# A hybrid mixer and mixture-of-experts layer on one core: one row load, wider matmul operands, other PSUM banks, and a new order of the last outputs

## The chip, the cores and the metric

The kernel runs on one core of one Trainium2 chip. The core has five engines that are told apart below: TensorE (PE; its weight loads are PEld), VectorE (DVE), ScalarE (ACT), GpSimd (POOL) and SyncE (SP), which here mostly issues DMAs. The metric is the device time of one execution, in microseconds; lower is better.

## The reference

The reference is one layer over 512 latent tokens and 256 context tokens, each of 1024 float32 numbers, written for a depth of 1 and a batch of 1:

- Modulation: `silu(c) @ ada_w + ada_b` gives six rows of 1024 (shift, scale and gate, twice); the context has its own.
- `xm = rmsnorm(x) * (1 + scale) + shift`, and one input projection `p = xm @ w_in` for all branches.
- Branch A: a bidirectional chunked state-space scan (16 heads, 4 groups, chunks of 128 tokens) over `silu(conv(p))`, started from the final states of the context. Its output gets the skip `y + d_skip[head] * xh`, is gated by `silu(z)` and normalised in groups of 256.
- Branch B: `u, v = gelu(uv)`; `v` is layer-normalised and mixed over 128 positions by `w_s`, then multiplied with `u`.
- `merged = sigmoid(gate_a) * (A @ w_pa) + sigmoid(gate_b) * (B @ w_pb)`, and `h = x + g1 * (merged @ w_o)`.
- `xf = rmsnorm(h) * (1 + scale2) + shift2`; each of 16 experts takes its 64 best tokens (`top_k` over a softmax of router logits), computes `silu(xg @ w_gate) * (xg @ w_up) @ w_down`, weighted by the affinity, and adds the result to its tokens: `h = h + g2 * sum`.
- The output is `rmsnorm(h) * final_norm_w`.

All weights are float32; the experts' alone are 16 x 3 x 4 MB = 201 MB.

## The kernel before, in words

**Order.** The work is written down stage by stage for all engines; a scheduler then turns it into one queue per engine, by the order of the program, by priorities and by when it reckons that operands are there. `keep_in_program_order` (the local `matmul` and `transpose`, L1042 to L1047) and `issue_after` (L1158) fix parts of TensorE's order by hand. A tile that is taken again under the same name waits until all that used its buffer is through; `bufs` gives the number of buffers.

**Start (L81 to L347).** POOL loads small rows through its own DMA queue (`vr`, `alog`, `dtb`, and `dsk`, L130: `d_skip` is spread so that partition p of column k has the value of head 2k + p // 64; each of the two loads takes every second of 16 numbers to 64 partitions). SP loads the tokens (L96), then `ada_w` and `w_in` tiles in turn. TensorE starts with `gemv(0)` (L237), which needs the first `ada_w` tile, then transposes the normalised tokens (L255) and projects group 0.

**Precision.** A float32 operand is split into a high and a low float32r part (`split`, L72: a ScalarE copy and a DVE subtraction); a product is three float32r matmuls (L358 to L360, L601 to L603). Products with plain float32 operands appear as two records each in the trace.

**Groups, v and u.** For groups 1 to 3 (L567) TensorE projects while the scan of the group before runs in steps (`ssd_group`, L446). The v half of branch B is projected with tokens on the partitions (`token_major`, L583): four blocks of 256 columns, each in two halves of four k, four token tiles with an accumulator each (`acc`, four banks), and an evacuation `v_out` (GELU by `gelu2`, L608, and `bn_stats`) after the second half. The statistics and the normalisation follow (L632 to L636). Then the scan's memory is given back, and in it `w_s` is loaded and transposed (L751, L760). The u half, the gates and the two branch projections follow (`cols`, `block`).

**Output projection.** `token_major` again (L951) with `w_o`; its evacuation `residual` (L916) multiplies with the gate into the buffer `t0` (one buffer), adds x into `h`, and squares with a sum. Between the halves stand the router's weights and the logits of each 256 columns (`logits`, L925). Softmax and ranking follow (L974 to L1039).

**Experts (L1127).** 16 experts run as 8 pairs, side by side in TensorE's columns. SP streams the weights in 1 MB tiles through 19 buffers (`expert_slots`, L645; `piece`, L687, takes one and issues more loads). Per pair: gate projection (tile `pg`, two PSUM banks), up projection (`pu`, two banks), the gather of the next pair's tokens (`channels`, L1074, two halves that share one tile of two banks, `pu` for the first pair and `pg` for the others), transposes through `x` (two banks), and the down projection in column cuts through `pd` (two banks). The result of a pair is spread to its tokens beside the next pair's gate projection (`to_their_tokens`, L1115).

**The end.** The last pair has cuts of 512, 384 and 128 columns (`LAST`, L29). Their results are spread through the four banks of `pg` and `pu`, the last cut's through `x` (`banks`, L1171); they are added to `h` and squared (L1190 to L1195, with junk output in two weight buffers). Then the final norm: `rsqrt` in nine small DVE steps (L132), `final_norm_w` spread over the partitions by eight matmuls with a broadcast column (L1230), and eight passes of 512 columns on DVE with a store each (L1237, L1238).

Of the kernel before, what the change touches and what calls it, by code (L numbers as in the profile page):

```python
# [18 lines left out]
GELU_K = 0.044715  # L19
# [9 lines left out]
LAST = ((0, 512, 4), (512, 896, 4), (896, 1024, 4))  # L29
# [4 lines left out]
def tile_backbone(  # L34
# [548 lines left out]
    def token_major(src, n0, lh, ll, evac, wt=lambda nb: wtile()):  # L583

        def weights():
            for nb in range(4):
                w = wt(nb).rearrange("p (k n) -> p k n", k=NK)
                load(w, w_cols(src, n0 + 256 * nb, 256))
                for kh in range(2):
                    wh, wl = hl_tile(4, 256)  # L590
                    wsplit(wh, wl, w[:, 4 * kh:4 * kh + 4, :])
                    yield nb, kh, wh, wl

        for nb, kh, wh, wl in ahead(weights()):
            if kh == 0:
                pp = [acc()[:, :256] for _ in range(NT)]
            for t in range(NT):
                for k in range(4):
                    kt = 4 * kh + k
                    a = slice(128 * t, 128 * t + 128)  # L600
                    T.matmul(pp[t], lh[:, kt, a], wh[:, k, :], start=kt == 0, stop=False)  # L601
                    T.matmul(pp[t], ll[:, kt, a], wh[:, k, :], start=False, stop=False)  # L602
                    T.matmul(pp[t], lh[:, kt, a], wl[:, k, :], start=False, stop=kt == NK - 1)  # L603
                if kh == 1:
                    evac(nb, t, pp[t])
            yield
# [12 lines left out]
    def v_out(nb, t, p):  # L619
        a = sp.tile([128, 512], F32, name="tm")[:, :256]  # L620
        gelu2(vt[:, t, 256 * nb:256 * nb + 256], p, a)
        if nb % 2:
            V.bn_stats(bn[:, t, nb // 2, :], vt[:, t, 256 * nb - 256:256 * nb + 256])

    for _ in token_major(W, 4128, xmh, xml, v_out):
        steps(scans, 2)
# [289 lines left out]
    def residual(nb, t, p):  # L916
        cs = slice(256 * nb, 256 * nb + 256)
        a = half("t0", 256)
        V.tensor_mul(a, p, g1b[:, cs])
        V.tensor_add(h[:, t, cs], a, x2[:, t, cs])  # L920
        S.activation(a, h[:, t, cs], AF.Square, accum_out=ssq[:, t, nb:nb + 1])
# [29 lines left out]
    for i, _ in enumerate(token_major(w_o.rearrange("l k n -> (l k) n"), 0, mgh, mgl, residual)):  # L951
        if i in {0:11}:
            fetch({0:11}[i])
        if i == 0:
            router_weights()
# [7 lines left out]
        elif i % 2 == 0:  # L963
            logits(i // 2 - 1)
    logits(3)
# [108 lines left out]
    def channels(xt_, ot, hf, p):  # L1074

        for j in range(4):
# [29 lines left out]
    first_banks = pw.tile([128, 2, 512], F32, name="pu", bufs=1)  # L1106
    for hf in range(2):
        channels(xg, ot, hf, first_banks[:, hf, :])
# [18 lines left out]
    for pr in range(NE // 2):  # L1127
# [15 lines left out]
        if not last:  # L1143
            gather = pw.tile([128, 2, 512], F32, name="pg", bufs=1)
            channels(xg, ot, 0, gather[:, 0, :])
# [6 lines left out]
        if not last:  # L1152
            channels(xg, ot, 1, gather[:, 1, :])
        def down(c0, c1, nk, behind=None):
            pd = pw.tile([128, 512], F32, name="pd", bufs=2)[:, :c1 - c0]
            for k0 in range(0, NK, nk):
                w = [piece() for _ in range(2)]
                with tc.issue_after(behind.ins) if behind and (k0 or c0 > 512) else nullcontext():  # L1158
                    for k in range(nk):
                        kt = k0 + k  # L1160
                        for e in range(2):
                            (T.matmul if last else matmul)(pd[64 * e:64 * e + 64, :], ht[:, kt, 64 * e:64 * e + 64], w[e][:, k, :],
                                     start=kt == 0, stop=kt == NK - 1)
# [7 lines left out]
        def banks(i):  # L1171

            if i == len(LAST) - 1:
                p = pw.tile([128, 512], F32, name="x").rearrange("p (t n) -> p t n", t=NT)
                return [p[:, t, :] for t in range(NT)]
            pp = [pw.tile([128, 2, 512], F32, name=n, bufs=1) for n in ("pg", "pu")]
            return [pp[t // 2][:, t % 2, :] for t in range(NT)]

        def scatter_last(i, a):

            c0, c1, _ = LAST[i]
            pp = banks(i)
            for t in range(NT):
                o = oh[:, 128 * t:128 * t + 128]
# [84 lines left out]
```

## Time and profile before

| | before |
|---|---|
| runs, us | 1151.94, 1154.35, 1153.66 (median 1153.66) |
| profiled execution, us | 1151.37 |
| its span, us | 1149.6 |
| mean granted TensorE clock | 0.989 |
| PE busy, us | 1070.2 (93%) |
| DVE / ACT / POOL busy, us | 579.2 / 331.9 / 66.2 |
| DMA | 291.85 MB, mean 254 GB/s |

The span runs from the first to the last instruction that the profiler saw; the execution's own time has some 2 us around it. Busy shares are averages over stages with different limits, so they are read stage by stage. The ends of matmuls are modelled; what a matmul takes in a stream is read from start to start.

### The profile page before, as it was taken

To read this page: it belongs to the slowest core of one execution; us is meant where nothing else is said; L and a number is where in the kernel's file an instruction comes from. 1 tells how busy PE (TensorE), PEld (TensorE's weight loads), DVE (VectorE), ACT (ScalarE), POOL (GpSimd) and SP (SyncE) were. 2 spreads that over 40 slices of the span, in tenths; PEclk is the share of its full clock that TensorE was granted. 3 is DMA by queue.
4 is the path that set the end of the run, shared out by engine and by line. 5 is a ranking of instruction groups with operands and counts; after the bars stand their busy time and mean duration, and the time that the engine had idled before them with its cause. 6 is when DMAs were issued, how large, how long until landed. Compare 5 with 4: busy or idle time off the path is not lost.

```text
span 1149.6 us, 15045 instructions
## 1 busy us (share of the span) xinstructions
PE 1070.2 (93%) x5939; PEld 709.5 (62%) x5939; DVE 579.2 (50%) x1061; ACT 331.9 (29%) x645; POOL 66.2 (6%) x58
## 2 busy tenths in 40 slices
PE   2999898999999999999999699999999999999985
PEld 1778777789888888777798545353535353535333
DVE  2768999998698565645653630303030303030305
ACT  4344756554343223323333211010101010101002
POOL 2002231321000000100000000000000000000000
PEclk9999999999999999999999799999999999999998
DMA  9941634231476566622464669999999999999994
GB/s 209 255 132 40 206 101 152 93 87 61 144 263 213 187 221 191 211 86 98 147 259 163 238 238 409 393 408 397 404 401 400 406 395 410 391 409 392 409 393 144
DMA packets 149663, 291.85 MB, mean 254 GB/s; under 512 B 8468, under 2 KB 75188, under 8 KB 149592
## 3 DMA queue, kind: packets, MB, share of 16 engines
q1 hardware_dynamic: 149224, 290.79, 70.5%
q0 software_dynamic: 288, 0.07, 0.7%
q8 instruction: 47, 0.77, 0.3%
q14 instruction: 24, 0.20, 0.1%
q10 hardware_dynamic: 80, 0.02, 0.0%
HBM read 288.67 MB, written 2.18 MB: 253 GB/s over the span
## 4 chain that ended last, share of the span: by engine, by line
PE 74%; DVE 11%; DMA 7%; ACT 4%; issue 3%; POOL 1%; SPq 0%; DVEq 0%; ACTq 0%; POOLq 0%
PE pg L1044 15%; PE pu L1044 10%; PE pd L1044 8%; PE acc L358 7%; PE acc L360 7%; PE acc L359 7%; PE x L1044 4%; PE acc L603 2%; PE acc L601 2%; PE acc L602 2%; DMA w<-in_w_up_dram 2%; DMA aw<-in_ada_w_dram 2%; DVE wl L74 1%; ACT m L1083 1%; DVE gq L515 1%
## 5 line engine op out<-in xcount | busy, mean ns | idle before, releaser
L358 PE MATMUL acc<-xmh,wh 128*128 128x512 f32 x352 | 139.0, 395 | 0.0
L359 PE MATMUL acc<-xml,wh 128*128 128x512 f32 x352 | 138.7, 394 | 0.0
L360 PE MATMUL acc<-xmh,wl 128*128 128x512 f32 x352 | 138.1, 392 | 0.0
L73 ACT CAST wh<-w 128x1024 fp32r<-128x1024 f32 (+1 forms) x84 | 84.4, 1006 | 170.4 <-PE acc L359 133.2
L74 DVE TENSOR_TENSOR wl<-w,wh 128x1024 fp32r<-128x1024 f32 (+1 forms) x81 | 96.3, 1190 | 68.0 <-ACT wh L73 66.8
L1168 DVE SCALAR_TENSOR_TENSOR t<-pd,gi,m 128x512 f32<-128x512 f32 (+2 forms) x17 | 12.2, 719 | 151.6 <-PE pd L1044 137.8
L1123 DVE TENSOR_TENSOR F<-F,x 128x512 f32<-128x512 f32 x56 | 38.5, 687 | 91.3 <-PE x L1044 91.3
L1044 PE MATMUL pg<-e,m 128*64 128x512 f32 x296 | 76.0, 602 | 0.0
L1044 PE MATMUL pu<-e,m 128*64 128x512 f32 x304 | 74.8, 595 | 0.9 <-DMA e<-in_w_up_dram 0.9
L360 PEld LDWEIGHTS acc<-xmh,wl 128*128 128x128 f32 x352 | 66.2, 188 | 14.8 <-issue 1.2
L358 PEld LDWEIGHTS acc<-xmh,wh 128*128 128x128 f32 x352 | 66.2, 188 | 14.6 <-ACT wh L73 0.8
L601 PE MATMUL acc<-wh,xmh 128*128 128x256 f32 x256 | 73.6, 288 | 1.0 <-DVE F L614 1.0
L359 PEld LDWEIGHTS acc<-xml,wh 128*128 128x128 f32 x352 | 66.3, 188 | 13.2 <-issue 0.4
L603 PE MATMUL acc<-wl,xmh 128*128 128x256 f32 x256 | 73.4, 287 | 0.6 <-DVE wl L74 0.6
L602 PE MATMUL acc<-wh,xml 128*128 128x256 f32 x256 | 72.6, 284 | 0.0
L1044 PE MATMUL pd<-e,m 128*64 128x512 f32 x280 | 66.6, 594 | 0.0
L1139 DVE TENSOR_TENSOR t<-t,pu 128x512 f32<-128x512 f32 x16 | 10.3, 683 | 99.6 <-PE pu L1044 99.6
L1083 ACT ACTIVATE m<-pg,mcol 128x128 f32<-128x128 f32 x56 | 21.0, 456 | 135.9 <-PE pg L1044 135.9
L1044 PEld LDWEIGHTS pg<-ot,F 128*128 128x128 f32 x448 | 51.1, 192 | 12.5 <-ACT m L1083 6.8
L1044 PE MATMUL pg<-ot,F 128*128 128x128 f32 x448 | 53.7, 279 | 5.1 <-ACT m L1083 5.1
L358 PE MATMUL acc<-rh,wh 128*128 128x512 f32 x128 | 50.4, 397 | 0.8 <-ACT rh L73 0.5
L603 PEld LDWEIGHTS acc<-wl,xmh 128*128 128x128 f32 x256 | 49.1, 192 | 3.4 <-issue 2.5
(401 smaller groups left out, 1911.8 us busy)
## 6 DMA issues: line engine op xcount, KB each, us to landing
e<-in_w_up_dram SPq DMA_DIRECT2D x38, 1024.0 KB
e<-in_w_gate_dram SPq DMA_DIRECT2D x37, 1024.0 KB
e<-in_w_down_dram SPq DMA_DIRECT2D x35, 1024.0 KB
w<-in_w_in_dram SPq DMA_DIRECT2D x23, 1024.0 KB
f<-in_w_down_dram SPq DMA_DIRECT2D x20, 1024.0 KB
f<-in_w_up_dram SPq DMA_DIRECT2D x19, 1024.0 KB
f<-in_w_gate_dram SPq DMA_DIRECT2D x19, 1024.0 KB
e<-in_ada_w_dram SPq DMA_DIRECT2D x32, 512.0 KB
```

The costliest lines, as they stand in the source:

```text
L73: S.copy(hi, src)
L74: (lo_eng or V).tensor_sub(lo, src, hi.bitcast(F32))
L358: T.matmul(p, wh[:, kt, :], rh[:, kt, :], start=kt == 0, stop=False)
L359: T.matmul(p, wh[:, kt, :], rl[:, kt, :], start=False, stop=False)
L360: T.matmul(p, wl[:, kt, :], rh[:, kt, :], start=False, stop=kt == NK - 1)
L601: T.matmul(pp[t], lh[:, kt, a], wh[:, k, :], start=kt == 0, stop=False)
L602: T.matmul(pp[t], ll[:, kt, a], wh[:, k, :], start=False, stop=False)
L603: T.matmul(pp[t], lh[:, kt, a], wl[:, k, :], start=False, stop=kt == NK - 1)
L1044: return tc.keep_in_program_order(T.matmul(*a, **k))
L1083: S.activation(xt_[:, k, :], p[:, 128 * j:128 * j + 128], AF.Identity, scale=mcol[:, 8 + k:9 + k], bias=mcol[:, k:k + 1])
L1123: V.tensor_add(h[:, t, c0:c0 + 512], h[:, t, c0:c0 + 512], p)
L1168: V.scalar_tensor_tensor(a, pd, gi[:, 0:1], g2k[:, c0:c1], op0=OP.mult, op1=OP.mult)
```

## The change

1. `d_skip` is loaded as one row of 16 numbers to all 128 partitions, and two POOL copies pick each half's numbers from it.
2. `token_major` takes a list of column cuts: `(0, 512), (512, 1024)` for v, and `(0, 512), (512, 768), (768, 1024)` for the output projection, there with `chained`: each matmul is issued after the one before it. A weight tile holds 2048 numbers a partition in either shape, and one split still has 1024.
3. `gelu2` does its inner polynomial in one DVE operation instead of two, with the constant in the scale of Tanh.
4. `residual` works in pieces of 256 columns and writes the squares over the PSUM operand.
5. `channels` takes a `pd` buffer for each half.
6. The last pair has cuts of 512, 256, 256 columns in a written order, each of the last two in two halves with outputs of the cut before between them; outputs go through `x` (two banks); squares are written over PSUM. `final_norm_w` is spread before the cuts, and h is multiplied by it piece by piece (`weigh`) before the final scale is known, except for the last 256 columns.
7. At the end DVE does the last 256 columns, ScalarE (DVE for the last token tile) scales the other 768, and each token tile is stored by one DMA from `h`.

```diff
-LAST = ((0, 512, 4), (512, 896, 4), (896, 1024, 4))
+LAST = ((0, 512, 4), (512, 768, 4), (768, 1024, 4))
...
+    dskr = sp.tile([128, 2 * NK], F32, bufs=1)
+    nc.gpsimd.dma_start(dskr, row_bc(d_skip, 0, 2 * NK))
     for s in range(2):
-        nc.gpsimd.dma_start(dsk[64 * s:64 * s + 64, :], dram(d_skip, s, [[0, 64], [2, NK]]))
+        g = slice(64 * s, 64 * s + 64)
+        G.tensor_copy(dsk[g, :], dskr[g, :].rearrange("p (k s) -> p s k", s=2)[:, s, :])
...
-    def token_major(src, n0, lh, ll, evac, wt=lambda nb: wtile()):
+    def token_major(src, n0, lh, ll, evac, cuts, chained=False):
...
+            for c0, c1 in cuts:
+                n = c1 - c0
+                nk, half_ = 2048 // n, 1024 // n
+                for k0 in range(0, NK, half_):
+                    if k0 % nk == 0:
+                        w = wtile().rearrange("p (k n) -> p k n", k=nk)
+                        load(w, dram(src, n0 + c0 + 128 * k0 * src.shape[1],
+                                     [[src.shape[1], 128], [128 * src.shape[1], nk], [1, n]]))
+                    wh, wl = hl_tile(half_, n)
+                    wsplit(wh, wl, w[:, k0 % nk:k0 % nk + half_, :])
+                    yield c0, c1, k0, half_, wh, wl
...
+                    for l_, w_ in ((lh, wh), (ll, wh), (lh, wl)):
+                        with tc.issue_after(behind.ins) if behind and chained else nullcontext():
+                            behind = T.matmul(pp[t], l_[:, kt, a], w_[:, k, :], start=kt == 0 and w_ is wh and l_ is lh,
+                                              stop=kt == NK - 1 and w_ is wl)
...
         S.activation(a, p, AF.Square)
-        V.tensor_scalar(a, a, GELU_C * GELU_K, GELU_C, op0=OP.mult, op1=OP.add)
-        V.tensor_mul(a, a, p)
-        S.activation(o, a, AF.Tanh)
+        V.scalar_tensor_tensor(a, a, 1.0 / GELU_K, p, op0=OP.add, op1=OP.mult)
+        S.activation(o, a, AF.Tanh, scale=GELU_C * GELU_K)
...
+            S.activation(p[:, ps_], h[:, t, cs], AF.Square, accum_out=ssq[:, t, nb:nb + 1])
...
-        elif i % 2 == 0:
-            logits(i // 2 - 1)
-    logits(3)
+        elif i > 3:
+            while done < ready_:
+                logits(done)
+                done += 1
+        ready_ = end // 256 if end else done
...
-    def channels(xt_, ot, hf, p):
-
+    def channels(xt_, ot, hf):
+
+        p = pw.tile([128, 512], F32, name="pd", bufs=2)
...
+        def add(i, t, c0, c1, p, square=True):
+
+            hc = h[:, t, c0:c1]
+            V.tensor_add(hc, hc, p)
+            if square:
+                S.activation(p, hc, AF.Square, accum_out=q[i][:, t:t + 1])
+            else:
+                V.scalar_tensor_tensor(p, hc, 1.0, hc, op0=OP.mult, op1=OP.mult, accum_out=q[i][:, t:t + 1])
+
+        def weigh(t, c0, c1):
+            hc = h[:, t, c0:c1]
+            V.tensor_mul(hc, hc, fnw[:, c0 // 512, c0 % 512:c0 % 512 + c1 - c0])
...
+            pd = down(a0, a1, ak)
+            _, hi, lo = halves_of(rp.tile([128, 512], F32R, name="t1"), rp.tile([128, 512], F32R, name="ya"), a0,
+                                  evac("t0", a0, a1, pd))
+            pd = down(b0, b1, bk, 4)
+            for t in range(NT):
+                p = pw.tile([128, 512], F32, name="x")
+                o = oh[:, 128 * t:128 * t + 128]
+                matmul(p, o, hi, start=True, stop=False)
+                matmul(p, o, lo, start=False, stop=True)
+                add(0, t, a0, a1, p)
+            down(b0, b1, bk, 4, pd)
+            yb = evac("t0", b0, b1, pd)
+            for t in range(NT):
+                weigh(t, a0, a1)
+            pd = down(c0, c1, ck, 4)
+            for t2 in range(0, NT, 2):
+                p = pw.tile([128, 512], F32, name="x").rearrange("p (t n) -> p t n", t=2)
+                for t in (t2, t2 + 1):
+                    matmul(p[:, t - t2, :], oh[:, 128 * t:128 * t + 128].bitcast(F32), yb, start=True, stop=True)
+                for t in (t2, t2 + 1):
+                    add(1, t, b0, b1, p[:, t - t2, :])
+            down(c0, c1, ck, 4, pd)
+            yc = evac("t1", c0, c1, pd)
+            for t in range(NT):
+                weigh(t, b0, b1)
...
+        V.scalar_tensor_tensor(h[:, t, cl:], h[:, t, cl:], r, fnw[:, 1, cl - 512:], op0=OP.mult, op1=OP.mult)
+        if t % 4 == 3:
+            V.tensor_scalar(h[:, t, :cl], h[:, t, :cl], r, None, op0=OP.mult)
+        else:
+            S.activation(h[:, t, :cl], h[:, t, :cl], AF.Copy, scale=r)
+        nc.sync.dma_start(outr[128 * t:128 * t + 128, :], h[:, t, :])
```

## Rows read from the trace of the kernel before

**Rows 1.** Windows: busy us (instructions) by engine, granted clock, DMA share, GB/s

```profile
0.00:20.00 20.00, 0.29 (x1) 0.18 (x1) 5.02 (x28) 8.17 (x12) 6.01 (x17) 1.00 0.91 171
20.00:40.00 20.00, 15.99 (x121) 12.19 (x121) 11.27 (x32) 8.55 (x18) 0.00 (x0) 1.00 0.85 242
...
660.00:680.00 20.00, 18.36 (x113) 9.53 (x113) 9.44 (x19) 3.22 (x9) 0.00 (x0) 1.00 0.40 148
680.00:700.00 20.00, 20.00 (x112) 9.33 (x109) 3.78 (x8) 1.78 (x3) 0.00 (x0) 1.00 1.03 403
...
1100.00:1120.00 20.00, 15.22 (x65) 5.06 (x66) 1.28 (x2) 1.17 (x2) 0.00 (x0) 1.00 1.05 388
```

**Rows 2.** Timeline, start: start us, us, engine, line, operation, names [idle, releaser]

```profile
12.33 2.19 ACT L226 ACTIVATE F<-F,rr 128x1024 f32<-128x1024 f32 x2 [2.02 <-DVE rr L143]
...
22.22 1.94 PE L237 MATMUL aux<-aw,scp 128*32 128x256 f32 x16 [14.48 <-DMA aw<-in_ada_w_dram]
...
25.57 5.29 PE L255 MATMUL aux<-ident,F 128*128 128x128 f32 x32
```

**Rows 3.** DMA view, 6 to 8 us, then 8 to 22: packets, MB, engine share

```profile
DMA packets 398, 0.78 MB, mean 392 GB/s; under 512 B 93, under 2 KB 223, under 8 KB 398
...
dsk<-in_d_skip_dram POOLq DMA_DIRECT2D x1, 2.0 KB, 15.3
...
q0 software_dynamic: 156, 0.02, 57.0%
q1 hardware_dynamic: 2606, 1.79, 42.0%
```

**Rows 4.** DMA view, queue q0, of 8 to 9 us and of 10 to 11 us

```profile
q0 software_dynamic: 56, 0.02, 35.9%
...
q0 software_dynamic: 13, 0.00, 271.0%
```

**Rows 5.** DMA issues, 0 to 25 us: KB each, median us to landing

```profile
alog<-in_a_log_dram POOLq DMA_DIRECT2D x1, 16.0 KB, 5.0
dtb<-in_dt_bias_dram POOLq DMA_DIRECT2D x1, 0.1 KB, 9.2
```

**Rows 6.** Timeline around the first expert pair

```profile
663.33 3.84 PE L1044 MATMUL pu<-ot,F 128*128 128x128 f32 x32 [1.64 <-ACT m L1083]
...
670.78 7.23 SPq L673 DMA_DIRECT2D e<-in_w_down_dram  x5
```

**Rows 7.** Timeline of TensorE, matmuls of 512 and of 256 columns

```profile
228.07 0.39 PE L358 MATMUL acc<-xmh,wh 128*128 128x512 f32 x1
...
231.24 0.39 PE L360 MATMUL acc<-xmh,wl 128*128 128x512 f32 x1
...
236.06 0.28 PE L603 MATMUL acc<-wl,xmh 128*128 128x256 f32 x1
...
241.45 0.28 PE L603 MATMUL acc<-wl,xmh 128*128 128x256 f32 x1
```

**Rows 8.** Lines by form, v stage, then end: busy us, mean ns

```profile
L611 DVE TENSOR_SCALAR tm<-tm 128x256 f32<-128x256 f32 x16 | 5.6, 349 | 0.2
...
L1190 DVE TENSOR_TENSOR F<-F,pg 128x512 f32<-128x512 f32 x2 | 1.3, 684 | 1.8 <-PE pg L1186 1.8
```

**Rows 9.** Timeline of TensorE at the wait for `w_s`

```profile
313.54 0.63 PE L760 MATMUL aux<-ident,e 128*128 128x128 f32 x4 [1.51 <-DMA e<-in_w_s_dram]
```

**Rows 10.** Timeline, last residual of the output projection

```profile
640.16 0.42 DVE L919 TENSOR_TENSOR t<-acc,m 128x256 f32<-128x256 f32 x1 [0.64 <-ACT t L921]
```

**Rows 11.** Timeline of the end, and two lines of its chain of waits

```profile
1118.51 3.65 PE L1162 MATMUL pd<-f,m 128*64 128x512 f32 x16 [1.57 <-DMA f<-in_w_down_dram]
...
1126.76 4.46 PE pd L1162 x28
...
1131.26 1.91 PE pd L1162 x28
...
1139.98 0.16 DVE L143 SCALAR_TENSOR_TENSOR rst<-rst 128x4 f32<-128x4 f32 x1
```

More of the change, by code (lines that the diff above doesn't have):

```diff
@@ L1104, in tile_backbone @@
     q = [fin[:, k, :] for k in range(8)]
[L1106 removed]
     for hf in range(2):
[L1108 removed]
+        channels(xg, ot, hf)
     def halves_of(hi, lo, c0, a):
@@ L1143, in tile_backbone @@
         if not last:
-            gather = pw.tile([128, 2, 512], F32, name="pg", bufs=1)
-            channels(xg, ot, 0, gather[:, 0, :])
+            channels(xg, ot, 0)
         for hf in range(2):
@@ L1152, in tile_backbone, with down @@
         if not last:
[L1153 to L1156, printed above, removed]
-                w = [piece() for _ in range(2)]
[L1158 to L1163, printed above, removed]
+            channels(xg, ot, 1)
+        def down(c0, c1, nk, k1=NK, pd=None):
+            k0, k1 = (NK - k1, NK) if pd is not None else (0, k1)
+            if pd is None:
+                pd = pw.tile([128, 512], F32, name="pd", bufs=2)[:, :c1 - c0]
+            for kk in range(k0, k1, nk):
+                w = [piece() for _ in range(2)]
+                for k in range(nk):
+                    kt = kk + k
+                    for e in range(2):
+                        matmul(pd[64 * e:64 * e + 64, :], ht[:, kt, 64 * e:64 * e + 64], w[e][:, k, :],
+                               start=kt == 0, stop=kt == NK - 1)
             return pd
@@ L1169, in evac @@
             return a
[L1171 to L1184, printed above, removed]
-                for j, b in enumerate(a):
-                    done = T.matmul(pp[t][:, :c1 - c0], o if len(a) > 1 else o.bitcast(F32), b,
-                                    start=j == 0, stop=j == len(a) - 1)
-            for t in range(NT):
-                hc = h[:, t, c0:c1]
-                V.tensor_add(hc, hc, pp[t][:, :c1 - c0])
-                j = junk[t % 2][:, :c1 - c0]
-                if i == 2 and t % 2:
-                    V.scalar_tensor_tensor(j, hc, 1.0, hc, op0=OP.mult, op1=OP.mult, accum_out=q[i][:, t:t + 1])
-                else:
-                    S.activation(j, hc, AF.Square, accum_out=q[i][:, t:t + 1])
-            return done
@@ L1211, in tile_backbone @@
-            yc = evac("t0", c0, c1, down(c0, c1, ck, first))
-            scatter_last(1, yb)
+            fnw = pw.tile([128, 2, 512], F32, name="pg", bufs=1)
+            for k in range(NK):
+                matmul(fnw[:, k // 4, 128 * (k % 4):128 * (k % 4) + 128],
+                       mcol[:, 24 + k:25 + k].to_broadcast([128, 128]), ident, start=True, stop=True)
+            pd = down(a0, a1, ak)
+            _, hi, lo = halves_of(rp.tile([128, 512], F32R, name="t1"), rp.tile([128, 512], F32R, name="ya"), a0,
+                                  evac("t0", a0, a1, pd))
@@ L1213, in tile_backbone @@
             V.tensor_add(q[0], q[0], q[1])
             V.tensor_scalar(q[0], q[0], 1.0 / 1024, EPS, op0=OP.mult, op1=OP.add)
-            scatter_last(2, (yc,))
+            for t2 in range(0, NT, 2):
+                p = pw.tile([128, 512], F32, name="x").rearrange("p (t n) -> p t n", t=2)
+                for t in (t2, t2 + 1):
+                    matmul(p[:, t - t2, :], oh[:, 128 * t:128 * t + 128].bitcast(F32), yc, start=True, stop=True)
+                for t in (t2, t2 + 1):
+                    add(2, t, c0, c1, p[:, t - t2, :], t % 2 == 0)
```

79 lines of the change are left out of this document (28 added, 51 removed).

## The prediction

> **What bounds the kernel now.** I read the page's slices first, then the windows of 20 us, the timelines and waits of the stages that the change touches, and the DMA view of the first 25 us. The span falls into three regimes.
>
> *The first 22 us wait for data.* TensorE does 0.29 us of work in the first 20 us [rows 1]. Its first stretch of matmuls (L237) starts at 22.22 after 14.48 us idle, released by the first `ada_w` tile; the tokens that the next PE work needs are normalised by 12.33 + 2.19 = 14.52 [rows 2]. The DMA moved 392 GB/s in 6 to 8 us, but SP's queue q1 only 1.79 MB in the whole of 8 to 22 us, with 42% of the engines, while 156 packets of POOL's queue q0 held 57% [rows 3]. In 10 to 11 us 13 of those packets held 271% of one microsecond of 16 engines, so some 43 engine-us, 3.3 us each [rows 4]. The heavy bursts belong to the two `d_skip` loads, 512 elements of 4 bytes each: the one issued in 6 to 8 us took 15.3 us to land, so until past 21, just before the `ada_w` tile [rows 2, 3], where `a_log`, from the same queue with 128 bytes a partition, landed in 5.0 [rows 5].
>
> *From there to about 656 TensorE sets the pace*, with few holes: after its start it is busy 15.99 of 20 us already at 20 to 40 [rows 1].
>
> *The expert stage is paced by the DMA from about 680 on*: share 1.03 at 403 GB/s, and TensorE down to 15.22 of 20 at 1100 to 1120 [rows 1]. But at 660 to 680 the DMA is only at 0.40 [rows 1]: every expert buffer is full, and SP goes on at 670.78, when TensorE has used the first tiles [rows 6]. So whatever TensorE gains before that moves the whole stream; what it gains afterwards the stream hides.
>
> **The change part by part.** The sum is made against the profiled execution (span 1149.6, 1151.37 us in all); the median of the runs lies 2.3 us above the latter.
>
> *Skip row.* Two loads of 512 four-byte pieces become one of 128 pieces of 64 bytes and two small POOL copies. POOL has nothing else to do at 20 to 40 us [rows 1], so the copies are free, even if they wait for the row. If q1 moves its 1.79 MB at 390 GB/s, it takes 4.6 us instead of 14: 9.4 us. Lower bound: only the engine time goes, 57% of 14 = 8.0 us, less what is added, 128 packets like those of 8 to 9 us (35.9% of 16 for 56, 0.10 us each, so 0.8 us over 16 engines [rows 4]), and as much for `dt_bias`, which stays: 6.4. Upper bound: the tokens are late next; the transposes (L255) go from 25.57 to 14.52 at best: 11.0 [rows 2]. I take 9.5, nearest to the measured rate. Later PE work is fed by the same queue, so all of it shifts together.
>
> By the Trainium skill (DMA: Bandwidth & Descriptors, Specifications) transfers under 512 bytes cost a read-modify-write, which speaks against a 64-byte row too. Taken per piece, an estimate from that rule leaves 128/1024 of the old 8.0, some 1.0 us, and the total gain would be about 13.2 instead of 14.2; the trace agrees so far as `d_skip`'s packets were slow, but `a_log`'s 128 bytes were not [rows 5].
>
> *v projection in 512 columns.* 384 matmuls of 256 columns become 192 of 512. Start to start, the 256-wide ones take (241.45 - 236.06)/45 = 0.120 us, the 512-wide (231.24 - 228.07)/14 = 0.226 [rows 7]: 192 x 0.013 = 2.5 us off TensorE. GELU loses one DVE pass per piece (16 x 0.35 = 5.6 us [rows 8]), but TensorE sets the pace there, so this is worth nothing by itself. Against it: four evacuations of 512 columns now fall together after the last matmul, some 2.1 us of DVE each (three passes near L1190's 0.68 [rows 8]) at 1.4 us spacing, so the normalisation (L636), which frees the memory of `w_s`, ends about 1 us later relative to TensorE, and TensorE already waits 1.51 for `w_s` [rows 9]. Net 1.5; bounds -1.0 (if the switch from the first cut to the second also stalls 2.5 us for a bank) and 3.
>
> By the skill (TensorE: Matmul & The Clock Gate, Back-to-back issue gap) a matmul of N columns takes N/2.4 GHz plus 2.5 ns, so merging two saves 2.5 ns, an estimate of 0.5 us here and 0.7 with the output projection. The rows differ, with 13 ns a pair; by the page's figure the total would be some 3 us smaller.
>
> *Output projection.* Half of it is widened: 96 x 0.013 = 1.3 us. The squares now go to PSUM, so the buffer `t0` is free after the addition: the last multiply, which waited 0.64 us for ScalarE [rows 10], starts some 0.3 earlier, and the last transposes with it. The chain fixes an order that the queue nearly has; logits 0 and 1 now come together behind the first part of the second cut, whose 48 matmuls (5.8 us) cover the additions they wait for. 1.6 in all; bounds -0.5 and 2.5.
>
> *Gather banks.* Before the first expert pair TensorE idles 1.64 us between the two gathers, until ScalarE has read the tile that both write [rows 6]; with a tile for each it doesn't, and the expert stream starts 1.6 us earlier. The same wait in each later pair is hidden by the DMA: nothing. Bounds 1.0 (if the second gather's bank still has a reader, DVE's ranking) and 1.7.
>
> *Last pair.* The bytes are the same, in runs of 1 KB instead of 1.5 and 0.5, and the second half of the first cut is waited for until 1118.51 [rows 11]. From the end of that cut (1118.51 + 3.65 = 1122.16) I lay out the new order with durations of the rows. The eight weight broadcasts stand ahead of the cut, in the wait for its data. First half of cut b: 16 records x 0.114 (256 columns, midway between 384 at 4.46/28 = 0.159 and 128 at 1.91/28 = 0.068 [rows 11]) to 1124.0. Outputs of a: only two banks now, each held through product, addition and square (0.7 each), so the last two wait some 1.6 us: to 1127.2. Second half of b to 1129.1, evacuated 1129.5; first half of c to 1130.9; outputs of b to 1131.9; second half of c to 1133.7, evacuated 1134.3. DVE gets four weighings near 0.68 and four near 0.42 in this part; where they stand in program order they hold the additions of b to 1132.2 to 1133.9, and those of c to 1136.4 to 1139.0; where they fall into gaps, c's end at 1137.3. Then the total and nine small steps of 0.2 to a result at 1139.3 to 1141.0; now L143 ends at 1140.14 [rows 11]. After it the passes shrink, from 1024 columns on DVE to 256, with 768 on ScalarE beside them, but the first store leaves no earlier, and in both versions 2 MB then have to be stored: the same end within 0.3. Last pair: 0, bounds -2 and +1.5.
>
> Sum: 9.5 + 1.5 + 1.6 + 1.6 + 0 = 14.2. Span 1135.4, profiled execution 1137.2, and from the median 1153.66 - 14.2 = **1139.5 us**.
>
> **The rivals.**
>
> *Half of the start.* The stall is not `d_skip`'s alone: `dt_bias` (32 pieces of 4 bytes, 9.2 us to landing [rows 5]) stays, and the new row adds 128 small pieces. Then the first tile comes only some 4.5 us earlier: 9.2 in all, 1144.5. For: `dt_bias` was slow. Against: it stood between the two `d_skip` loads in the same queue.
>
> *A costly last pair.* The two banks and the weighings put the result 5 us later than now: 1144.5 as well. For: DVE has 4.4 us more to do in the last 12. Against: most of it fits where DVE waits for TensorE.
>
> *Nothing passes on.* The expert stream would be bound by its own start, because tiles loaded before 660 land late: all but what comes of the last pair is lost, 1153.7. Against: share 0.40 at 660 to 680 [rows 1].
>
> *Slower.* The cost is per packet of q0, not per element. Then 128 packets of the broadcast row at 3.3 us hold 16 engines for 26 us where the present bursts hold 8: the start is 18 us later, the rest gains 4.7, and the time is 1167. It decides from 1.6 us a packet on (128 x 1.6 / 16 = 12.8, about 8.0 + 4.7). Against: 56 packets at 0.10 us in 8 to 9 us [rows 4] and `a_log`'s 5.0.
>
> **How the numbers follow.** Forecast (10 to 18 us gained) 0.76; half of the start 0.11; costly last pair 0.07; nothing passes on 0.03; slower 0.03. The range: 1134.5 is all terms near their upper bounds (11.0 + 3 + 2.5 + 1.7 + 1), 1146.5 takes in the two partial cases at 1144.5 and 2 us for the spread of the runs. A measurement of this kernel tells about 0.2% (2.3 us) from no change: faster 0.94, same 0.03, slower 0.03.
>
> **What would show it.** L237's first matmul at 12 to 13 us and no packet of 3 us on q0; the work up to the v stage 9 to 10 us earlier; that stage about 2 us shorter on TensorE, with a longer wait for `w_s`; no wait for L1083 ahead of the second gather; SP's first expert load after its pause at about 656.5; the same time from there to the last weight tile; and some 18 us, within 2, from the end of the last pair's first cut to the end of the nine small steps. The forecast is wrong if the first `ada_w` tile still lands after 17 us, or if the shift of the start is not found again at 656.

## The result, and the profile after

The changed kernel takes 1141.16 us (median of 4 runs, 1139.69 to 1143.87), the kernel before 1154.01 us on the same chip (4 runs): ratio 0.9894, 95% interval [0.9871, 0.9917]. In a second set of runs the ratio was 0.9889 [0.9870, 0.9907]. The profiled execution took 1141.62 us, its span 1139.6, so 10.0 less than the span before. The forecast was 1139.5 and a gain of 14.2; the medians lie 12.9 apart. Its terms, though, came out quite differently, and partly with the other sign.

The windows that answer to [rows 1], with those of 100 to 120 and 640 to 660 us added (columns as in [rows 1]: busy us and instructions of PE, PEld, DVE, ACT, POOL, then granted clock, DMA share, GB/s):

```profile
0.00:20.00 20.00, 6.91 (x39) 5.53 (x40) 7.16 (x34) 12.25 (x21) 5.52 (x18) 1.00 0.97 309
20.00:40.00 20.00, 19.79 (x158) 14.97 (x157) 16.78 (x46) 8.46 (x17) 0.00 (x0) 1.00 0.83 235
100.00:120.00 20.00, 19.15 (x104) 16.28 (x103) 15.95 (x36) 11.31 (x30) 8.62 (x6) 0.91 0.74 188
...
640.00:660.00 20.00, 14.27 (x92) 10.74 (x92) 18.59 (x43) 3.11 (x9) 0.00 (x0) 0.75 0.54 204
660.00:680.00 20.00, 20.00 (x106) 7.42 (x104) 3.70 (x7) 1.99 (x4) 0.00 (x0) 1.00 0.98 369
```

TensorE has 6.91 us of work in the first 20 us instead of 0.29, and the DMA is already at 0.98 at 660 to 680, where it was at 0.40. New is a granted clock of 0.91 at 100 to 120. The DMA view of 8 to 22 us answers to [rows 3], and the issues of 0 to 25 us to [rows 5] (KB each, median us to landing):

```profile
q1 hardware_dynamic: 7257, 4.69, 107.3%
q0 software_dynamic: 136, 0.03, 3.9%
...
alog<-in_a_log_dram POOLq DMA_DIRECT2D x1, 16.0 KB, 5.7
dskr<-in_d_skip_dram POOLq DMA_DIRECT2D x1, 8.0 KB, 6.5
dtb<-in_dt_bias_dram POOLq DMA_DIRECT2D x1, 0.1 KB, 6.1
```

SP's queue moved 4.69 MB there instead of 1.79; `dt_bias` landed in 6.1 us instead of 9.2. The timelines that answer to [rows 2], [rows 6], [rows 9] and [rows 10]:

```profile
12.86 1.93 PE L240 MATMUL aux<-aw,scp 128*32 128x256 f32 x16 [5.20 <-DMA aw<-in_ada_w_dram]
16.20 6.46 PE L258 MATMUL aux<-ident,F 128*128 128x128 f32 x32
...
306.58 0.63 PE L767 MATMUL aux<-ident,e 128*128 128x128 f32 x4 [1.36 <-DMA e<-in_w_s_dram]
...
593.23 0.42 DVE L927 TENSOR_TENSOR t<-acc,m 128x256 f32<-128x256 f32 x1 [0.64 <-ACT acc L929]
...
596.01 1.22 DVE L74 TENSOR_TENSOR wl<-w,wh 128x1024 fp32r<-128x1024 f32 x1 [0.91 <-ACT wh L73]
...
598.69 0.39 PE L612 MATMUL acc<-wh,xmh 128*128 128x256 f32 x1 [1.68 <-ACT acc L929]
...
601.07 0.39 PE L612 MATMUL acc<-wh,xmh 128*128 128x256 f32 x1 [0.46 <-ACT acc L929]
...
631.48 0.42 DVE L927 TENSOR_TENSOR t<-acc,m 128x256 f32<-128x256 f32 x1 [0.55 <-PE acc L612]
...
647.24 8.63 PE L1058 MATMUL pd<-ot,F 128*128 128x128 f32 x64
...
659.48 7.23 SPq L680 DMA_DIRECT2D e<-in_w_down_dram  x5
```

The first `ada_w` product starts 9.36 us earlier, both gathers are one run of 64 matmuls, and SP goes on 11.30 earlier (14.3 were forecast). In the output projection TensorE now waits 1.68 + 0.46 us for an accumulator bank that ScalarE still writes; before, no matmul of that stage waited for a bank. The last multiply, [rows 10], now waits for TensorE alone. The end, which answers to [rows 11]:

```profile
1111.05 0.75 DVE L1183 SCALAR_TENSOR_TENSOR t<-pd,gi,m 128x512 f32<-128x512 f32 x1 [9.63 <-PE pd L1058]
...
1115.33 0.50 PE L1058 MATMUL x<-t,ot 128*128 128x512 f32 x1 [1.13 <-ACT x L1191]
...
1120.20 1.99 PE L1058 MATMUL x<-t,ot 128*128 128x256 f32 x8
1121.37 0.42 DVE L1189 TENSOR_TENSOR F<-F,x 128x256 f32<-128x256 f32 x1 [1.70 <-PE x L1058]
...
1124.12 0.49 DVE L1183 SCALAR_TENSOR_TENSOR t<-pd,gi,m 128x256 f32<-128x256 f32 x1
...
1130.80 0.16 DVE L146 SCALAR_TENSOR_TENSOR rst<-rst 128x4 f32<-128x4 f32 x1
1130.99 2.59 ACT L1258 ACTIVATE F<-F,rst 128x768 f32<-128x768 f32 x3 [3.21 <-DVE rst L146]
```

From the end of the last pair's first cut, where its evacuation starts, to the end of the nine steps it is 1130.96 - 1111.05 = 19.9 us, before 1140.14 - 1122.16 = 18.0.

### The profile page after: what moved, and what is told of

It is laid out like the page before. It is cut to its first block, busy times and chain, and to the rows that moved or that the text cites. A ratio compares the mean times of both kernels' runs of the same rounds, so it can differ in the third digit from the quotient of the medians.

```text
span 1139.6 us, 14368 instructions
## 1 busy us (share of the span) xinstructions
PE 1073.7 (94%) x5651; PEld 698.8 (61%) x5651; DVE 570.6 (50%) x1025; ACT 332.2 (29%) x631; POOL 66.5 (6%) x59
## 4 chain that ended last, share of the span: by engine, by line
PE 75%; DVE 9%; DMA 9%; issue 2%; ACT 2%; POOL 1%; SPq 0%; ACTq 0%; DVEq 0%; POOLq 0%
PE pd L1058 13%; PE pg L1058 9%; PE pu L1058 8%; PE acc L361 8%; PE acc L612 8%; PE acc L362 8%; PE acc L363 8%; PE x L1058 4%; DMA w<-in_w_up_dram 2%; DMA e<-in_w_gate_dram 2%; DMA e<-in_w_up_dram 2%; DMA w<-in_w_gate_dram 1%; PE aux L537 1%; DVE gq L518 1%; PE x L1061 1%
## 5 line engine op out<-in xcount | busy, mean ns | idle before, releaser
L1183 DVE SCALAR_TENSOR_TENSOR t<-pd,gi,m 128x512 f32<-128x512 f32 (+1 forms) x17 | 12.2, 720 | 140.5 <-PE pd L1058 140.5
L362 PEld LDWEIGHTS acc<-xml,wh 128*128 128x128 f32 x352 | 66.4, 189 | 12.8
L1058 PE MATMUL pd<-e,m 128*64 128x512 f32 (+1 forms) x328 | 72.2, 563 | 0.0
L1098 ACT ACTIVATE m<-pd,mcol 128x128 f32<-128x128 f32 x64 | 24.1, 457 | 147.4 <-PE pd L1058 147.4
L1058 PEld LDWEIGHTS pd<-ot,F 128*128 128x128 f32 x512 | 59.6, 195 | 5.9 <-issue 5.9
L1058 PE MATMUL pd<-ot,F 128*128 128x128 f32 x512 | 61.7, 280 | 0.0
L612 PE MATMUL acc<-wh,xmh 128*128 128x512 f32 (+1 forms) x160 | 56.7, 354 | 2.1 <-ACT acc L929 2.1
L612 PE MATMUL acc<-wl,xmh 128*128 128x512 f32 (+1 forms) x160 | 56.1, 351 | 0.0
L612 PE MATMUL acc<-wh,xml 128*128 128x512 f32 (+1 forms) x160 | 55.9, 349 | 0.0
L1058 PEld LDWEIGHTS pu<-e,m 128*64 128x64 f32 x304 | 26.2, 137 | 44.6 <-issue 35.9
```

The costliest lines, as they stand in the source:

```text
L362: T.matmul(p, wh[:, kt, :], rl[:, kt, :], start=False, stop=False)
L612: behind = T.matmul(pp[t], l_[:, kt, a], w_[:, k, :], start=kt == 0 and w_ is wh and l_ is lh, stop=kt == NK - 1 and w_ is wl)
L1058: return tc.keep_in_program_order(T.matmul(*a, **k))
L1098: S.activation(xt_[:, k, :], p[:, 128 * j:128 * j + 128], AF.Identity, scale=mcol[:, 8 + k:9 + k], bias=mcol[:, k:k + 1])
L1183: V.scalar_tensor_tensor(a, pd, gi[:, 0:1], g2k[:, c0:c1], op0=OP.mult, op1=OP.mult)
```

## The experiments

To see where time goes, the same instructions were laid side by side: for each kernel, the median shift in us against the profiled execution before, over the DVE, ACT and PE instructions with the same source text that start in the 15 us from the time at the head of the column (times of before). The seventh column is the first cut of the last pair (L1168), the last the span. "old" is a part put back as before.

| kernel | 90 | 210 | 390 | 570 | 630 | 690 | last pair | span |
|---|---|---|---|---|---|---|---|---|
| changed, first profile | -9.1 | -6.5 | -11.1 | -10.9 | -8.7 | -11.3 | -11.1 | -10.0 |
| changed, again | -9.1 | -10.0 | -14.8 | -13.6 | -11.4 | -13.5 | -13.3 | -12.2 |
| before + row | -9.2 | -7.4 | -7.4 | -7.2 | -7.1 | -7.4 | -7.3 | -7.3 |
| old `d_skip` loads | -0.7 | +2.4 | -2.0 | -0.7 | +1.5 | -0.6 | -0.5 | +0.7 |
| old squares | -8.9 | -9.9 | -15.2 | -15.1 | -12.4 | -14.0 | -14.0 | -13.0 |
| old end | -9.0 | -10.0 | -14.9 | -11.9 | -9.6 | -12.6 | -12.6 | -12.5 |
| old output projection | -9.1 | -9.9 | -14.9 | -13.3 | -13.2 | -15.8 | -15.6 | -14.4 |
| unchained | -9.2 | -10.2 | -15.0 | -13.5 | -14.0 | -16.3 | -16.3 | -15.3 |
| old output projection, old end | -9.2 | -9.7 | -14.0 | -11.8 | -11.7 | -13.6 | -13.6 | -13.5 |
| old GELU, wide v | -8.5 | -7.5 | -10.0 | -9.2 | -7.0 | -8.6 | -8.4 | -7.3 |
| before + row + short GELU | -9.0 | -10.0 | -10.5 | -8.5 | -8.5 | -8.7 | -8.9 | -8.8 |
| one strided load | -5.9 | -6.9 | -11.7 | -11.1 | -8.9 | -10.6 | -10.5 | -9.3 |
| unchained, old end | -9.3 | -8.2 | -13.6 | -10.4 | -10.9 | -12.8 | -12.8 | -12.5 |

**The start.** The kernel before with the new row alone, and the changed kernel with the old loads:

```diff
-    for s in range(2):
-        nc.gpsimd.dma_start(dsk[64 * s:64 * s + 64, :], dram(d_skip, s, [[0, 64], [2, NK]]))
+    dskr = sp.tile([128, 2 * NK], F32, bufs=1)
+    nc.gpsimd.dma_start(dskr, row_bc(d_skip, 0, 2 * NK))
+    for s in range(2):
+        ...
+        G.tensor_copy(dsk[g, :], dskr[g, :].rearrange("p (k s) -> p s k", s=2)[:, s, :])
```

> Kernel before with the skip row alone (one 64-byte row to 128 partitions and two POOL copies). Theory 1: the stall of the first 22 us was the packets of the two 4-byte loads, and nothing else in the change touches the start: L237's first matmul goes from 22.22 to 12.9, as in the changed kernel, and the work from 108 us on stands 6.5 to 9.4 us earlier; the upper figure if TensorE's granted clock stays at 1.0, the lower if it falls to 0.57 in 100 to 104 and 124 to 128 us as it did in the changed kernel. Time 1144.6 to 1147.5. Theory 2 (half of the start): the other pieces of the change, or dt_bias's 32 small pieces, had a part in it: 1149 or more.

> Changed kernel with the two 4-byte loads of d_skip put back. Theory 1: the start is 9.4 us later again, but the dips of the granted clock between 100 and 128 us, which the kernel before doesn't have, go too, since TensorE's work there stands where it stood before: loss 6.5 to 7.5 us, 1147.7 to 1148.7. If the dips stay, they belong to something else in the change: loss 9.4, 1150.6. Theory 2 (rival: the later stages can give part of the start back, because the expert stream has slack): loss under 5 us, under 1146.

The row alone: 1143.68 against 1151.66 us, ratio 0.9929 [0.9911, 0.9947]. Its first product starts at 12.91, and the shift of 9.2 at 90 us goes through to the end but for 1.9 lost in between, all but 0.1 of it by 210 us, after a dip of the clock at 100 to 103: theory 1, though its time is 0.9 below the range given. With the old loads in the changed kernel: 1150.99, ratio 0.9983 [0.9967, 1.0000], so nearly all the gain is gone, as theory 1 has it where the dips stay (1150.6); the expert stream gives nothing of the start back, and the rival falls. But the dips of the clock didn't go with the row: this kernel starts where the one before does and has two as well, at 108 and 132.

**One strided load.** In the changed kernel the lower half of the tile comes by the old load again:

```diff
+    nc.gpsimd.dma_start(dsk[0:64, :], dram(d_skip, 0, [[0, 64], [2, NK]]))
-    for s in range(2):
+    for s in range(1, 2):
```

> Changed kernel in which the upper half of d_skip's tile comes from the row, and the lower half by the old load of 512 four-byte elements: one such load in place of two or none. Theory 1: the stall is the time that these elements hold the 16 DMA engines, so in proportion to their number: L237's first matmul at 17.4 us, midway between 12.9 and 22.0; the time 4 to 5 us above the changed kernel. Theory 2 (rival): the two loads held the engines beside one another, or one alone is enough to stop SP's queue: the first matmul at 20 us or later. Theory 3: one load fits into the time before ada_w is needed: under 14.5.

Median 1141.69, ratio 0.9917 [0.9897, 0.9937]. The DMA view of 8 to 22 us, then TensorE's timeline:

```profile
q1 hardware_dynamic: 4317, 3.13, 68.9%
q0 software_dynamic: 150, 0.03, 36.3%
```

```profile
12.85 1.93 PE L241 MATMUL aux<-aw,scp 128*32 128x256 f32 x16 [5.25 <-DVE F L232]
20.63 4.26 PE L259 MATMUL aux<-ident,F 128*128 128x128 f32 x20 [1.64 <-DVE mod L248]
```

The engine time follows the number of elements: in this trace the load's 16 packets of 32 elements took 3.84 us each, so 3.8 us of all 16 engines; before, the two loads' 32 packets took 3.79 each, 7.6 in all. (The 36.3% hold 1.2 us of another row's packets as well.) The delay doesn't: the first product still starts at 12.85, because this load stands behind the row in POOL's queue, and its packets start at 11.9 to 13.0 and run to some 17.8, where they meet the tiles after the first. The loss at 90 us is 3.2, a third of 9.1 and not the forecast half. The start at 12.85 is in theory 3's range, but the load did not fit in ahead of the tile: it came after it. None of the three theories gave the place.

**The dips.** The changed kernel was run once more:

> The changed kernel once more, on the chip of the other three, as what they are compared with. If the dips of TensorE's granted clock at 100 and 124 us in its first trace belong to this program, they are there again, and the shift against the kernel before at 180 us is -6.5; if they come by chance from one execution to the next, the shift is anything from -6.5 to -9.9 (without dips, as in two other kernels with the same code up to 229 us).

Windows of 4 us of the first profile, then of the second:

```profile
100.00:104.00 4.00, 4.00 (x20) 3.35 (x19) 1.33 (x4) 0.55 (x2) 1.69 (x2) 0.57 0.54 140
124.00:128.00 4.00, 4.00 (x30) 3.67 (x28) 2.74 (x4) 4.00 (x12) 0.00 (x0) 0.57 0.43 124
```

```profile
100.00:104.00 4.00, 4.00 (x31) 3.61 (x30) 2.24 (x5) 1.14 (x3) 2.06 (x2) 1.00 0.58 147
124.00:128.00 4.00, 3.94 (x23) 3.15 (x22) 3.79 (x7) 3.43 (x9) 2.91 (x2) 1.00 0.95 316
```

The same program had its clock mostly at the lower level, 1.2 GHz, in both windows of one execution, with 20 matmuls for 31, and at 2.4 GHz in the other. The work at 210 us stands 3.5 us apart. So the dips do not belong to the program, and all shifts in the column of 210 carry them. The chip may have a part in it, but on one chip too the mean granted clock of the kernel before goes from 0.985 to 0.990 from run to run. The spread of the runs goes with it: of 39 runs of the kernel before, the 8 with a mean granted clock of 0.987 took 1153.7 us on average, the 6 at 0.990 took 1149.5. Times that differ by 2 us are therefore better read from the shifts of a stage than from medians.

**The output projection.** Three versions of the changed kernel: the squares in SBUF again; no fixed order; and the four narrow cuts of before (with squares in SBUF as well).

```diff
-            S.activation(p[:, ps_], h[:, t, cs], AF.Square, accum_out=ssq[:, t, nb:nb + 1])
+            S.activation(a, h[:, t, cs], AF.Square, accum_out=ssq[:, t, nb:nb + 1])
```

> Changed kernel with the squares of the residual written to the SBUF tile t0 again, not to the accumulator's bank. Theory 1: the 2.1 us that the output projection lost between 583 and 633 us are TensorE's waits for an accumulator bank that ScalarE still writes (L612 <- L929, 1.68 and 0.46 us): they go, the pick of the first pair and the expert stream come 2 us earlier, 1139.1. Theory 2 (rival): the wait is only moved: t0 is then held by ScalarE, VectorE's multiply waits for it as before, and the bank comes free no earlier: within 0.6 of 1141.2. Theory 3: the loss is the chained order with the interleaved logits, and squares have no part in it: the waits for ScalarE go, but the stage stays as long: within 0.6 of 1141.2.

```diff
-                                        ((0, 512), (512, 768), (768, 1024)), chained=True)):
+                                        ((0, 512), (512, 768), (768, 1024)))):
```

> Changed kernel without the fixed order in the output projection; its three cuts of 512, 256 and 256 columns and all else stay. Theory 1 (the wide cut's banks cost the time): other matmuls of the stage can step ahead while one waits for a bank, but all of the cut's matmuls want the same banks, so the shift at 633 stays within 1 us of the changed kernel's. Theory 2 (rival: the fixed order costs the time): L612's waits for a bank go, the shift at 633 is 2.2 us better, the time 2.2 lower.

```diff
-                                        ((0, 512), (512, 768), (768, 1024)), chained=True)):
+                                        ((0, 256), (256, 512), (512, 768), (768, 1024)))):
...
-        elif i > 3:
-            while done < ready_:
-                logits(done)
-                done += 1
+        elif i % 2 == 0:
+            logits(i // 2 - 1)
```

> Changed kernel with the output projection as before: four cuts of 256 columns, no fixed order, squares into t0, logits one by one. Theory 1: the new form lost 2.2 us there (the shift against the kernel before goes from -10.8 at 583 to -8.7 us at 633), because four evacuations of 512 columns fall behind one another and the second cut's matmuls wait for their banks. With four narrow cuts no matmul of the stage waits for a bank, the shift stays as it was at 583, and the expert stream starts 2.2 us earlier: 2.2 us under the changed kernel. Theory 2 (rival): routing behind the stage is bound by other work (the clock's low stretch from 636 on, VectorE's picks), which takes the 2.2 us up: the same as the changed kernel within 0.7.

What TensorE waits for at 575 to 640 with the old squares (us in total, times, longest), then the two longest of the unchained kernel at 583 to 632:

```profile
PE acc L612 <- DVE t L927: 1.4, 2, 0.7
PE aux L939 <- DVE F L928: 1.1, 3, 0.7
```

```profile
PE aux L947 <- ACT m L943: 0.6, 1, 0.6
PE aux L939 <- DVE F L928: 0.3, 1, 0.3
```

Squares: ratio 0.9911 [0.9886, 0.9935], no gain, and the stage loses 2.6 us from 570 to 630 instead of 2.2. The wait for the bank has only changed hands, from ScalarE to VectorE's multiply, which waits 0.64 for ScalarE again: theory 2. Theory 3 forecast the same time, and the next version bears out its cause, the fixed order. Without the fixed order no matmul waits for a bank, and the stage gains 0.6 us where the chained one loses 2.2; the ratio, 0.9876 [0.9857, 0.9896], can't be told from the changed kernel's 0.9889 on the same chip. Theory 1 (all matmuls want the same banks) falls: in the 10 us from the second cut's first matmul (592.37 and 594.97) the unchained kernel starts 62 of the stage's matmuls, the chained one 39, because the next weight block's products into a bank that is already free step ahead of the wait (at 594.15 to 595.87). With the narrow cuts (0.9878 [0.9859, 0.9898], no clearer) the shift stays, -13.3 and -13.2, and goes on to 690: theory 1 there, and the routing doesn't take the time up.

**The last pair.** The changed kernel with the end of before (its `LAST`, `down`, `banks`, `scatter_last` and final passes in place of the new ones), then together with the narrow output projection, and together with the unchained one:

```diff
-LAST = ((0, 512, 4), (512, 768, 4), (768, 1024, 4))
+LAST = ((0, 512, 4), (512, 896, 4), (896, 1024, 4))
```

> Changed kernel with the end of the kernel before: last pair in 512, 384 and 128 columns, its four banks, halves and scatter, norm weights and final passes as they were. Theory 1: the new order of the last pair costs 2.0 us from the end of its first cut to the end of the nine small steps (18.0 to 19.9), and its shorter output passes give 0.8 back: net 1.2, 1140.0. Theory 2 (rival): the steps are 2 us longer only because the last weights came at another moment against TensorE; with the old end in the same place the time is the same within 0.5, 1141.2.

> Changed kernel with both parts undone that cost time by its trace: the output projection of the kernel before, and the last pair and final passes of the kernel before. What remains is the skip row, the wide v projection with its shorter GELU, and the gather banks. Theory 1: the two gains add, 2.2 + 1.2: 3.4 us under the changed kernel, some 15 to 16 us under the kernel before. Theory 2 (rival): the last pair's loss hangs on when its weights come; with the stream 2.2 us earlier the old end gives nothing more: 2.2 under the changed kernel.

> Changed kernel without the fixed order in the output projection (its wide first cut stays) and with the last pair and final passes of the kernel before. Theory 1: both losses go and add: the stage from 583 to 633 gains 0.6 instead of losing 2.1, the stretch from the last pair's first evacuation to the end takes 27.45 us instead of 28.5: 3.8 us under the changed kernel, 0.6 under the version with the narrow output projection. Theory 2 (rival): the expert stream is bound by its transfers, and TensorE's gain before it is not all passed on: within 1 us of the kernel with the fixed order left out alone.

From the last pair's first evacuation to the end of the span it is 27.4 us before and 27.5, 27.5 and 27.7 in these three; with the new end 28.6, and 28.4 to 28.6 in the six other kernels that have it. So the new end costs 1.1 us wherever the stream stands: theory 1 of the first two. By ratio the old end alone, 0.9886 [0.9866, 0.9905], can't be told from the changed kernel. Both losses undone with narrow cuts give the fastest kernel here: 1135.15 us, 0.9852 [0.9831, 0.9874], its runs 1134.36 to 1137.87 beside 1137.78 to 1142.38 of the changed kernel on the same chip. The unchained one with the old end came to 1138.80, 0.9881 [0.9862, 0.9900]. Its runs had a low clock (0.985 to 0.990), and its stages are as theory 1 has it (-10.4 to -10.9 from 570 to 630, 27.7 at the end, and the shift of 12.8 at 690 is still there at the last pair). Its time alone, 0.6 below the unchained kernel's 1139.43 on another chip, would fit theory 2 as well; which of the two is better is not settled.

**The v projection.** Wide with the old GELU, and narrow with the short one:

```diff
-        V.scalar_tensor_tensor(a, a, 1.0 / GELU_K, p, op0=OP.add, op1=OP.mult)
-        S.activation(o, a, AF.Tanh, scale=GELU_C * GELU_K)
+        V.tensor_scalar(a, a, GELU_C * GELU_K, GELU_C, op0=OP.mult, op1=OP.add)
+        V.tensor_mul(a, a, p)
+        S.activation(o, a, AF.Tanh)
```

> Changed kernel with the GELU of the kernel before (multiply-add, product, tanh: one VectorE pass more for each piece) in the wide v projection. Theory 1: VectorE's passes are hidden beside TensorE there, as the prediction said; the 4.8 us that the work between 225 and 345 us gains on the kernel before are the wide matmuls: the gain stays within 0.7 of 4.8. Theory 2 (rival): part of it is the shorter GELU, which in the kernel before let a matmul wait 1.0 us for a bank and 0.6 for a split weight; with four long evacuations behind one another TensorE waits for banks at the change of cuts: the gain falls to 2.5 or less, the time is 2 to 4 us above the changed kernel.

> Kernel before with the skip row and the short GELU, but v in four cuts of 256 columns. Theory 1: the width makes the gain of the v projection; with the short GELU alone the work from 225 to 345 us gains only the waits for a bank (1.0) and a split weight (0.6), at most 1.6 us against the kernel with the skip row alone. Theory 2 (rival): the gain is VectorE's passes: 3 us or more.

Of TensorE's waits, without those for `w_s` and for the scan: at 236 to 325 before, then at 225 to 375 of the wide v projection with the old GELU:

```profile
PE acc L601 <- DVE F L614: 1.0, 1, 1.0
PE acc L603 <- DVE wl L74: 0.6, 1, 0.6
```

```profile
PE acc L361 <- ACT wh L73: 0.6, 1, 0.6
PE acc L362 <- DVE rl L74: 0.6, 1, 0.6
PE acc L612 <- DVE F L624: 0.4, 1, 0.4
```

From 210 to 390 the changed kernel gains 4.8 us (4.6 in its first profile, 4.4 to 5.3 in the eight others with the same stage). Width alone keeps 2.4, but in the v projection it gains 4.2: the shift goes from -7.5 at 210 to -11.7 by 330, stays there up to 362 us, and loses 1.8 by 375. That loss is at the end of the u half, which uses `gelu2` too (L781 of the changed kernel), so that both versions change it there as well: TensorE waits 0.59 and 0.61 us, at 357.31 and 359.10 of that trace, for operands that VectorE and ScalarE split late. In v the old GELU costs one wait of 0.4 for a bank. The short GELU alone gains 0.5: the two waits of before are gone, but one of 0.9 for VectorE at L529 is new, and that for `w_s` is 1.8. The ratios agree: 0.9928 [0.9909, 0.9948], some 4 us above the changed kernel, and 0.9917 [0.9898, 0.9935]. By its figures theory 2 of the first holds, but most of the loss is not at the change of cuts; theory 1 of the second holds: width makes the gain, and the short GELU keeps it through the u half.

## Why the prediction was right in sum, and where not

| term | forecast | measured |
|---|---|---|
| skip row | -9.5 | -9.1 to -9.4 |
| v projection, with the u half's GELU | -1.5 | -4.8 |
| output projection | -1.6 | +2.2 |
| gather banks | -1.6 | -2.0 |
| last pair and output | 0 | +1.1 |
| granted clock and the rest | 0 | +0.4 (second profile), +3.0 (first) |

Measured is the second profile, without dips: -9.1 - 4.8 + 2.2 - 2.0 + 1.1 + 0.4 = -12.2. Its last term is -0.9 from 90 to 210 us, +1.2 from 390 to 570 and +0.1 in the expert stage; that of the first is +2.5, +0.3 and +0.2. That the sum came out is in part luck: v and u gave 3.3 us more than forecast, the output projection 3.8 and the last pair 1.1 less.

*Skip row: right, with its mechanism.* q0's long packets are gone, q1 moves more than the forecast needed, and the work after it shifts together. The rivals that put the cost on `dt_bias` or on packets fall: 136 packets of q0 now hold 3.9% of 14 us of 16 engines, 0.06 us each, less than the 0.10 reckoned with. The row came in 16 packets of 512 bytes, not in the 128 that the bound and the rival took, and they took 0.04 us each. By the Trainium skill (DMA: Bandwidth & Descriptors, Specifications) transfers under 512 bytes do a read-modify-write, and an estimate from that made the sum 13.2. In this trace the row's 64-byte pieces show no such cost beside 3.3 us for a packet of four-byte elements [rows 4].

*v projection: the mechanism of the cost was wrong.* The 2.5 us of width are there. The step that the normalisation "ends about 1 us later relative to TensorE, and TensorE already waits 1.51 for `w_s`" failed. Its last lines, before and after:

```profile
305.74 2.98 DVE L636 TENSOR_SCALAR F<-F,mv,r 128x1024 f32<-128x1024 f32 x4
```

```profile
298.69 1.53 DVE L643 TENSOR_SCALAR F<-F,mv,r 128x1024 f32<-128x1024 f32 x2
```

It ends at 300.22 instead of 308.72, 8.5 us earlier, and 2.0 earlier against the work at 210 (0.1 later with the old GELU). The wait came to 1.36, and to 1.0 in the second profile (0.8 with the old GELU, where the first `w_s` matmul starts 4.5 us after the load's issue instead of 6.2; why is open). That a DVE pass less is "worth nothing by itself" was nearly right, 0.5 us; but the forecast left out that the u half has the same GELU, where it is worth 1.8 once v is wide. And before, TensorE waited 1.0 for a bank and 0.6 for a split weight in the v stage; these waits stood in the trace, and the forecast didn't count them. Width and the short GELU together leave no such wait, in v or u. 2.5 for width + 1.0 + 0.6 + 0.5 for `w_s` is 4.6 of the 4.8.

*Output projection: the sign was wrong, outside its bounds.* "The chain fixes an order that the queue nearly has" is the step that failed. It was true of four narrow cuts, where no matmul waits for a bank. After a cut of 512 columns four long evacuations stand behind one another, each of four VectorE passes of 0.42 us and two squares, and into the second of them falls the split of the next weights: VectorE idles 0.91 us for ScalarE's half of it and takes 1.22 for its own, at 596.01. The second cut's second token tile needs the bank of that evacuation and waits 1.7 for it, and the chain holds the next weight block's products, which could run meanwhile, behind that wait. The unchained kernel has the same split in the same place and doesn't wait, so it is the order that costs. The same stall had been priced at 2.5 us as a bound for v, where it did not come, and was left out here. The squares' move did what was forecast: from the start of the last matmul to that of the last multiply it is 0.31 us (631.17 to 631.48), and 0.66 both before and with the squares in SBUF again, and the stage loses 0.4 less by it. What it did not do is free a bank sooner: the waits for one are 2.1 us with it and 1.4 without.

*Gather banks: right.* The 1.64 wait is gone; 1.6 to 3.0 us were gained from 630 to 690 in the kernels with the change, 0.2 in the two without it. It varies with the clock, which comes back from its lower level, 1.2 GHz, while the gathers run (0.76 at 648 to 652 in the first profile). From the first gather's start to the last one's end it is 11.0 to 11.3 us in the three profiles without the change, of which 3.7 to 4.2 at the lower level, and 8.3 to 9.7 in the eleven with it, of which 2.0 to 5.0. Less half of the time at the lower level, that is 9.1 to 9.2 in each of the three and 7.2 to 7.3 in each of the eleven: the change is worth 1.9 at the same clock, and the clock makes the rest of the spread.

*Later pairs: right, and better to be seen than expected.* Waits in the expert stage, before at 700 to 930, then after at 1000 to 1070:

```profile
PE pg L1044 <- ACT m L1083: 2.9, 4, 0.8
```

```profile
PE pu L1058 <- DMA e<-in_w_up_dram: 2.4, 2, 1.5
```

A pair took 58.46 us before and takes 57.48 after, without the 0.7 at each gather, so the lead grows from 12.3 us at the first pair's first evacuation to 16.7 at the sixth's. From there TensorE waits for weights, and at the last pair's it is 11.1, as SP's restart was 11.3 earlier: all that TensorE gained inside the stage is given back.

*Last pair: within its bounds, 1.1 above the value.* The layout to the end of the nine steps, 17.1 to 18.8 us by its own figures, came out at 19.9. The wait for a bank until ScalarE has squared is 1.13 us, less than the 1.6 reckoned with. What was mis-sized are the products themselves: the outputs of a take 4.0 us with that wait (1112.66 to 1116.68) for 3.2, and those of b 1.99 in 8 records of 0.25 for 1.0. So the second half of b and what follows come later, and VectorE idles 1.70 at 1121.37 before the first sum of b. The step "the same end within 0.3" erred the other way: nine steps to the end take 8.6 us, before 9.5, with ScalarE's three passes (2.59) beside VectorE's.

*The clock* was not in the forecast. The two dips put the first profile's work at 210 us 3.5 us behind the second's, and make most of the difference between spans 10.0 and 12.2 us shorter.

## What to carry to other kernels

A load of many four-byte elements at the head of a kernel is paid by every other queue; fetch the row whole and pick on chip. A helper that two stages share has to be reckoned in both. An order written out by hand is right for one tiling: when a cut doubles, count the banks and the evacuations behind one another before fixing the order, or leave it free. And read a change of many parts by the shift of the same instructions from stage to stage: a sum can come out right with one term a third of its size and another of the wrong sign.

## What the runs showed of the hardware

TensorE's granted clock fell to 0.57 over a stretch of 4 us in some executions and not in others of the same program, at 100, 108, 124, 132 and 460 us. In the first profile TensorE had idled 1.74 of 4 us at 96 to 100 and 1.96 at 120 to 124, just before its two; in the second it idles 1.72 at 96 to 100 and keeps 1.00. What decides was not found. Between 390 and 570 us the kernels without a dip there lose 0.1 to 1.6 us. It is one wait, of TensorE for the sum of a modulation on VectorE (L742 of the changed kernel), which itself follows the `ada_w` tiles: 1.5 us before, 1.6 to 3.1 in these, and the loss is this wait less 1.5 in each, within 0.1. Why it varies stays open.
